# Compression blocks split straight from PSUM, and two element-wise steps moved to ScalarE

## Chip, cores, metric

One core of a Trainium2 chip. The metric is the device time of one execution in microseconds (us), the median over executions. TensorE (PE), VectorE (DVE), ScalarE (ACT), GpSimd (POOL) and SyncE (SP) each work through their own instruction list in order and wait for one another by semaphores; SP and ACT also start DMA transfers.

## What is computed

One layer of a hybrid transformer on 512 tokens of width 1024, all in float32. A mixer (sparse attention with compressed, selected and window branches, beside an mLSTM) is followed by cross-attention to 256 memory tokens and a SwiGLU network. The part around the change:

```python
def compress_blocks(kv, pos, w1, w2):               # blocks of 32 positions, stride 16
    c = kv.reshape(B, H, S // 16, 16, DH)           # 31 blocks come of 512 positions
    blocks = jnp.concatenate([c[:, :, :-1], c[:, :, 1:]], axis=3) + pos
    hid = jax.nn.silu(blocks.reshape(B, H, -1, 32 * DH) @ w1)
    return hid @ w2

def hybrid_mixer(h, ...):
    (nq, kc, vc, ksl, vsl, kwn, vwn, gt, mq, mk, mv, mi, mf, mo) = jnp.split(h @ w_in, IN_OFFSETS, axis=-1)
    k_cmp = compress_blocks(kv_heads(kc), cmp_pos_k, cmp_w1_k, cmp_w2_k)
    v_cmp = compress_blocks(kv_heads(vc), cmp_pos_v, cmp_w1_v, cmp_w2_v)
    o = native_sparse_attention(q, k_cmp, v_cmp, ...)
    qk = silu(causal_depthwise_conv([mq, mk], conv_w, conv_b))   # 4 taps
    hm = mlstm_chunkwise(mq, mk, mv, mi, log_sigmoid(mf))        # 4 heads
    hm = rms_norm_per_head(hm) * mlstm_norm
    y_ml = sigmoid(mo) * hm
    return jnp.concatenate([y_nsa, y_ml], axis=-1) @ w_out
```

## The kernel before

A float32 product is made of three matmuls of parts: each operand is split into a high part (a ScalarE copy, L166) and a low part (a subtraction, L167, on VectorE or GpSimd), and `mm3` (L292 to L295) multiplies low by high, high by low and high by high.

The in-projection h @ w_in is made in tiles of 128 output columns by 512 tokens. `dense_tiles` takes for each a PSUM bank of the tag "d" (`bk_dT`), of which there are **two**, runs 24 matmuls of 512 columns into it (8 slices of depth, three each), and hands the bank to an evacuation function. Its weights are split for two tiles at a time into `whi` and `wlo`. The order in which tiles and other work are written is a string of the table PLAN, and it begins

```python
"order": "c0 Lk c0 Lv kc m0 m0 Ck Ck Ck Ck c1 kc S0 O0 c1 S1 Cv Cv Cv Cv m2 S2 m2 O2 ks O1 ks q0 S3 q0 O3",
```

Here c0 and c1 are pairs of tiles for the convolution, kc is the pair of tiles of the compression's keys and values (the first kc is k, the second v), m0 and m2 are the output gate's tiles, Ck and Cv quarters of the compression's first product, S and O the scores and outputs of an mLSTM head. A scheduler of the framework then fixes the order of each engine's list and gives each tile its bank; a bank that is taken again waits until its last reader is done. What the engines carry out is that fixed order.

The functions that the change touches, by the line numbers of the profile:

- `ev_conv` (L654 to L667) evacuates a tile of the convolution: ScalarE copies the bank to `u` (L659), VectorE makes the first tap `zc = u*w3 + b` (L660) and adds three shifted taps (L663); ScalarE takes tanh (L665), VectorE finishes the silu (L666).
- `ev_mo` (L669 to L675) evacuates the output gate: ScalarE takes tanh from the bank (L673, `sg`), VectorE makes (sg + 1) * gain (L674).
- `ev_kcvc` (L751 to L770) builds the compression's blocks: two zeroed tiles `Xr`, eight additions of the positions from the bank (L761, 64 x 8 x 31 each), and four splits of `Xr` into `Xb` (L166, L167). The block dimension has 32 columns for 31 blocks, the last left zero.
- `comp` (L821 to L835) multiplies `Xb` by the split weights `w1s` (L830, 16 matmuls of 512 columns into `bk_hb`); `comp_out` (L837 on) adds two halves of the result through a matmul with the constant `fold`.

`mlstm_scores` (L687 to L718) stands beside them: it stacks q and k (`qm`, `kmA`, `kmB`), fetches a row broadcast over the partitions by a DMA that ScalarE starts (`rb`, L697), lets GpSimd add the causal mask (`dg`, L699), and ScalarE takes ten exponentials of pieces of `rb` and `dg` (L714, `sT`), which VectorE multiplies with the scores (L716). Later, `compressed` (L616 to L650) makes the softmax `pc` of the compressed branch on VectorE from PSUM and the bias tiles `nB`, which are fetched by DMA into tiles that the scores `sT` held before.

Of the kernel before, what the change touches and what calls it, by code (L numbers as in the profile page):

```python
# [8 lines left out]
F32 = mybir.dt.float32  # L9
F32R = mybir.dt.float32r  # L10
AF = mybir.ActivationFunctionType
OP = mybir.AluOpType
AX = mybir.AxisListType

P = 128
# [31 lines left out]
def hybrid_layer(ctx, tc, a, out):  # L47
# [39 lines left out]

# [34 lines left out]
    def engines(name):  # L122
        return [ENG[c] for c in PLAN[name]]
# [13 lines left out]
    def slot(shape, dt=F32, name="slot"):  # L137
        return sl.tile(shape, dt, tag="S", name=name)

    def gran(shape=(P, 512), dt=F32, name="gran"):  # L140
        return gp.tile(list(shape), dt, tag="G", name=name)
# [7 lines left out]
    def sgran(shape=(P, 512), dt=F32, name="s"):  # L149
        return gp.tile(list(shape), dt, tag="s", name=name, bufs=8)  # L150
# [10 lines left out]
    def small(shape, name, bufs=2):  # L161
        return sm.tile(shape, F32, tag=name, name=name, bufs=bufs)

    def split(hi, lo, src, eng=None, scale=None):
        if scale is None:
            first = nc.scalar.activation(hi, src, AF.Copy)  # L166
            second = (eng or nc.vector).tensor_tensor(lo, src, hi.bitcast(F32), op=OP.subtract)  # L167
        else:
            first = nc.scalar.activation(hi, src, AF.Copy, scale=scale)
            second = nc.vector.scalar_tensor_tensor(lo, src, scale, hi.bitcast(F32), op0=OP.mult, op1=OP.subtract)  # L170
        return first.ins, second.ins
# [277 lines left out]
    def cw(c, w):  # L449
        return chan[:, 4 * w + c:4 * w + c + 1]  # L450

    def cb(c):
        return chan[:, 16 + c:17 + c]

    def hn(c):
        return chan[:, 20 + c:21 + c]
# [197 lines left out]
    def ev_conv(base):  # L654
        def f(j, b):
            c = base + j
            u = gran(name="u")
            y = zc[c] = gran(name="zc")
            nc.scalar.activation(u, b, AF.Copy)  # L659
            nc.vector.tensor_scalar(y, u, cw(c, 3), cb(c), op0=OP.mult, op1=OP.add)  # L660
            for w in range(3):
                d = 3 - w
                nc.vector.scalar_tensor_tensor(y[:, d:512], u[:, 0:512 - d], cw(c, w), y[:, d:512],  # L663
                                               op0=OP.mult, op1=OP.add)
            nc.scalar.activation(u, y, AF.Tanh, scale=0.5)  # L665
            nc.vector.scalar_tensor_tensor(y, u, 1.0, y, op0=OP.add, op1=OP.mult)  # L666
        return f  # L667

    def ev_mo(base):  # L669
        def f(j, b):  # L670
            c = base + j
            sg[c] = gran(name="sg")
            nc.scalar.activation(sg[c], b, AF.Tanh, scale=0.5)  # L673
            nc.vector.tensor_scalar(sg[c], sg[c], 1.0, hn(c), op0=OP.add, op1=OP.mult)  # L674
        return f  # L675


# [71 lines left out]
    Xb = {}  # L749

    def ev_kcvc(j, b):  # L751
        n = "kv"[j]
        Xr = [sgran((P, 8, 64), name="Xr") for _ in range(2)]
        for X in Xr:
            nc.gpsimd.memset(X, 0.0)
        for kv in range(2):
            for r in range(2):
                full = b[64 * kv:64 * kv + 64, :].rearrange("p (b j r) -> p r j b", r=2, j=8)
                pt = posT[n][64 * r:64 * r + 64, :]
                for q in range(2):  # L760
                    nc.vector.tensor_tensor(Xr[q][64 * r:64 * r + 64, :, 32 * kv:32 * kv + 31],  # L761
                                            full[:, r, :, q:q + 31],
                                            pt[:, 8 * q:8 * q + 8].rearrange("p (j o) -> p j o", o=1).to_broadcast([64, 8, 31]),
                                            op=OP.add)
        Xb[n] = []
        for X in Xr:
            for g in range(2):
                B = gran((P, 4, 2, 64), F32R, name="Xb")
                split(B[:, :, 0, :], B[:, :, 1, :], X[:, 4 * g:4 * g + 4, :], engines("xb")[g])
                Xb[n].append(B)  # L770

    def dup(A, src, s=1.0):
        for r in (0, 64):
# [37 lines left out]
    hb, w1r = {}, {}  # L811
    fold = cst.tile([P, 64], F32, name="fold")
    nc.vector.tensor_tensor(fold, ident[:, 0:64], ident[:, 64:128], op=OP.add)

    def comp_load(n, g):
        w1r[n, g] = [ygran((P, 2, 256), name="w1") for _ in range(4)]
# [4 lines left out]
    def comp(n):  # L821

        hb[n] = bank("sc", "bk_hb")
        for s in range(8):
            take = x4 if PLAN["w1t" + n][s] == "T" else w4
            w = take([P, 2, 2, 256], F32R, name="w1s")
            split(w[:, :, 0, :], w[:, :, 1, :], w1r[n, s // 4][s % 4], engines("w1" + n)[s])
            for k in range(2):
                kk = 2 * s + k
                nc.tensor.matmul(hb[n], lhsT=Xb[n][kk // 4][:, kk % 4].rearrange("p q b -> p (q b)"),  # L830
                                 rhs=w[:, k].rearrange("p q c -> p (q c)"), start=kk == 0, stop=kk == 15)
            if s == 7:
                comp_out(n)
            if s % 2:
                yield  # L835
# [567 lines left out]
```

## Time and profile before

| | |
|---|---|
| median of 3 runs | 849.34 us (847.7, 849.34, 850.01) |
| the profiled execution's own time | 851.17 us |
| its span in the profile | 849.4 us |
| outside the span | 1.8 us |
| PE, DVE, ACT, POOL busy in the span | 819.2, 545.8, 422.3, 302.0 us |
| mean granted clock of TensorE | 0.992 of full speed |

The profiled execution is 1.8 us above the median of the runs. In the rows of the profile, a line number is that of the kernel before, `out<-in` are the program's names, and idle time is the engine's own, with what ended it. Matmuls overlap, so one that lasts 0.39 us may follow the one before by 0.23 us.

### The profile page before, as it was taken

The numbers are of one execution on the slowest core, as the hardware profiler recorded it, in microseconds if no ns is written. First come the engines' busy times: TensorE is split into PE (matmuls) and PEld (weight loads), VectorE is DVE, ScalarE is ACT, GpSimd is POOL, SyncE is SP. The second block draws the span as 40 slices with busy tenths as digits, with TensorE's granted clock in tenths as the row PEclk, the third lists the DMA queues.
The fourth block names the chain that finished last, engine by engine and source line by source line (L and its number), as shares of the span: only waits on it lengthen the run. The fifth ranks groups of instructions, "written<-read, shape, count | busy, mean of one in ns | idle before, by whom it ended". The sixth has DMA issues, their size and how long they took to land.

```text
span 849.4 us, 12651 instructions
## 1 busy us (share of the span) xinstructions
PE 819.2 (96%) x4841; PEld 703.4 (83%) x4841; DVE 545.8 (64%) x933; ACT 422.3 (50%) x837; POOL 302.0 (36%) x224
## 2 busy tenths in 40 slices
PE   8999989998999999999999999999999999999997
PEld 5776767885688978778888889999999999888885
DVE  6639596688879835743453769988877885224423
ACT  5513565757867743743452556444444444324311
POOL 3223342255437542411320111444444444323420
PEclk9999998999999999999999999999999999999999
DMA  8372222421202232251441033333333322223102
GB/s 260 109 226 73 62 66 70 136 69 51 66 11 88 91 137 84 60 189 50 141 155 51 1 124 103 118 113 110 114 113 112 110 104 100 100 100 99 50 25 75
DMA packets 67763, 83.18 MB, mean 98 GB/s; under 512 B 4368, under 2 KB 53873, under 8 KB 67702
## 3 DMA queue, kind: packets, MB, share of 16 engines
q1 hardware_dynamic: 64574, 77.97, 28.5%
q10 hardware_dynamic: 3128, 4.40, 1.6%
q8 instruction: 38, 0.62, 0.3%
q14 instruction: 23, 0.19, 0.1%
HBM read 80.24 MB, written 2.12 MB: 97 GB/s over the span
## 4 chain that ended last, share of the span: by engine, by line
PE 81%; DVE 10%; ACT 5%; issue 2%; POOL 1%; DMA 0%; DVEq 0%; ACTq 0%; POOLq 0%; SPq 0%
PE bk_X L1251 5%; PE bk_X L1252 5%; PE bk_X L1253 5%; PE bk_dT L293 5%; PE bk_ff L294 5%; PE bk_ff L295 5%; PE bk_ff L293 5%; PE bk_dT L294 5%; PE bk_dT L295 5%; PE bk_pv L977 3%; PE bk_dN L294 3%; PE bk_dN L293 3%; PE bk_dN L295 3%; PE bk_Z L1251 2%; PE bk_Z L1253 2%; PE bk_Z L1252 2%
## 5 line engine op out<-in xcount | busy, mean ns | idle before, releaser
L166 ACT ACTIVATE whi<-raw 128x1024 fp32r<-128x1024 f32 (+1 forms) x80 | 76.8, 967 | 66.6 <-PE bk_dT L293 28.4
L167 DVE TENSOR_TENSOR wlo<-raw,whi 128x1024 fp32r<-128x1024 f32 x41 | 55.9, 1367 | 78.4 <-PE bk_ff L294 43.0
L167 POOL TENSOR_TENSOR wlo<-raw,whi 128x1024 fp32r<-128x1024 f32 x23 | 55.9, 2429 | 102.2 <-ACT whi L166 100.3
L166 ACT ACTIVATE wh<-raw 128x1024 fp32r<-128x1024 f32 x64 | 67.2, 1056 | 49.5 <-PE bk_X L1251 17.8
L167 POOL TENSOR_TENSOR wl<-raw,wh 128x1024 fp32r<-128x1024 f32 x19 | 55.5, 2919 | 97.3 <-ACT wh L166 69.9
L293 PE MATMUL bk_dT<-hTh,wlo 128*128 128x512 f32 x192 | 77.5, 404 | 2.3 <-DVE Xr L761 1.1
L294 PE MATMUL bk_dT<-hTl,whi 128*128 128x512 f32 x192 | 76.7, 400 | 0.0
L295 PE MATMUL bk_dT<-hTh,whi 128*128 128x512 f32 x192 | 76.5, 398 | 0.0
L167 DVE TENSOR_TENSOR wl<-raw,wh 128x1024 fp32r<-128x1024 f32 x45 | 65.6, 1464 | 9.4 <-ACT wh L166 9.4
L167 POOL TENSOR_TENSOR gs<-gf,gs 128x512 fp32r<-128x512 f32 x22 | 33.6, 1536 | 64.7 <-ACT gs L166 64.7
L1252 PE MATMUL bk_X<-A,wh 128*128 128x256 f32 x192 | 54.6, 284 | 1.0 <-DVE A L167 1.0
L1251 PE MATMUL bk_X<-A,wl 128*128 128x256 f32 x192 | 54.4, 283 | 0.4 <-ACT A L166 0.4
L1253 PE MATMUL bk_X<-A,wh 128*128 128x256 f32 x192 | 54.3, 283 | 0.0
L294 PE MATMUL bk_ff<-wlo,gs 128*128 128x512 f32 x128 | 49.8, 389 | 0.0
L295 PE MATMUL bk_ff<-whi,gs 128*128 128x512 f32 x128 | 49.6, 389 | 0.0
L1251 PE MATMUL bk_X<-AS,wl 128*128 128x256 f32 x160 | 45.6, 285 | 2.7 <-ACT u L1306 2.6
L293 PE MATMUL bk_ff<-whi,gs 128*128 128x512 f32 x128 | 47.4, 389 | 0.0
L293 PEld LDWEIGHTS bk_dT<-hTh,wlo 128*128 128x128 f32 x192 | 36.5, 190 | 11.7 <-DVE wlo L167 2.1
L947 POOL TENSOR_SCALAR s<-s,acf 128x128 f32<-128x128 f32 (+3 forms) x32 | 36.3, 1146 | 25.6 <-PE bk_tr L962 15.9
L1252 PE MATMUL bk_X<-AS,wh 128*128 128x256 f32 x160 | 44.9, 281 | 0.0
L1253 PE MATMUL bk_X<-AS,wh 128*128 128x256 f32 x160 | 44.9, 281 | 0.0
L1251 PE MATMUL bk_Z<-AS,wl 128*128 128x256 f32 x160 | 44.9, 281 | 0.0
(374 smaller groups left out, 2533.3 us busy)
## 6 DMA issues: line engine op xcount, KB each, us to landing
raw<-in_w_gate_up_dram SPq DMA_DIRECT2D x22, 1024.0 KB, 5.7
raw<-in_w_down_dram SPq DMA_DIRECT2D x11, 1024.0 KB, 5.0
raw<-in_w_xkv_dram SPq DMA_DIRECT2D x8, 1024.0 KB, 5.1
raw<-in_w_in_dram SPq DMA_DIRECT2D x7, 1024.0 KB, 5.4
raw<-in_w_out_dram SPq DMA_DIRECT2D x4, 1024.0 KB, 5.1
raw<-in_w_xq_dram SPq DMA_DIRECT2D x4, 1024.0 KB, 5.2
raw<-in_w_xo_dram SPq DMA_DIRECT2D x4, 1024.0 KB, 5.1
raw<-in_w_in_dram SPq DMA_DIRECT2D x6, 512.0 KB, 4.0
```

Source lines behind the costliest of these rows:

```text
L166: first = nc.scalar.activation(hi, src, AF.Copy)
L167: second = (eng or nc.vector).tensor_tensor(lo, src, hi.bitcast(F32), op=OP.subtract)
L293: nc.tensor.matmul(o, lhsT=wl, rhs=xh, start=start, stop=False)
L294: nc.tensor.matmul(o, lhsT=wh, rhs=xl, start=False, stop=False)
L295: return nc.tensor.matmul(o, lhsT=wh, rhs=xh, start=False, stop=stop).ins
L947: ENG[on].tensor_scalar(s[:, 0:n], s[:, 0:n], c, None, op0=OP.mult)
L977: nc.tensor.matmul(o, lhsT=v, rhs=pTs[br][q][:, j], start=(br, j, q) == mms[0], stop=(br, j, q) == mms[-1])
L1251: nc.tensor.matmul(o, lhsT=wl[:, k, c], rhs=A.hi(n, k), start=st, stop=False, skip_group_check=True)
L1252: nc.tensor.matmul(o, lhsT=wh[:, k, c], rhs=A.lo(n, k), start=False, stop=False, skip_group_check=True)
L1253: nc.tensor.matmul(o, lhsT=wh[:, k, c], rhs=A.hi(n, k), start=False, stop=stop and k == 3, skip_group_check=True)
```

## The change

In the compression, `Xr` and its additions go. The bank itself is split: a view of it with overlapping blocks (31 columns at a stride of 16) is copied by ScalarE and subtracted by VectorE, 64 x 16 x 31 at a time, four of each for k and four for v, into one tile `Xb` from the pool `slot`. The positions are split into column 31, that of the missing block, and `fold` gets its row of that column added to all its columns, so that the positions' product reaches every block in the matmul that was there already. The first tap of the convolution and the scale of the output gate become activations on ScalarE. TensorE's matmuls are the same in number and shape. Line numbers behind the table are lower by 1, those behind `ev_kcvc` by 5.

```diff
--- before.py
+++ after.py
@@ -85,7 +85,6 @@
         "w1tk": "WTWTWTWW",
         "w1tv": "WWWWWWWW",
 
-        "xb": "vv",
         "c0": "pp",
         "c1": "vp",
         "m0": "pp",
@@ -657,7 +656,7 @@
             u = gran(name="u")
             y = zc[c] = gran(name="zc")
             nc.scalar.activation(u, b, AF.Copy)
-            nc.vector.tensor_scalar(y, u, cw(c, 3), cb(c), op0=OP.mult, op1=OP.add)
+            nc.scalar.activation(y, b, AF.Identity, scale=cw(c, 3), bias=cb(c))
             for w in range(3):
                 d = 3 - w
                 nc.vector.scalar_tensor_tensor(y[:, d:512], u[:, 0:512 - d], cw(c, w), y[:, d:512],
@@ -671,7 +670,7 @@
             c = base + j
             sg[c] = gran(name="sg")
             nc.scalar.activation(sg[c], b, AF.Tanh, scale=0.5)
-            nc.vector.tensor_scalar(sg[c], sg[c], 1.0, hn(c), op0=OP.add, op1=OP.mult)
+            nc.scalar.activation(sg[c], sg[c], AF.Identity, scale=hn(c), bias=hn(c))
         return f
 
 
@@ -749,25 +748,18 @@
     Xb = {}
 
     def ev_kcvc(j, b):
+
         n = "kv"[j]
-        Xr = [sgran((P, 8, 64), name="Xr") for _ in range(2)]
-        for X in Xr:
-            nc.gpsimd.memset(X, 0.0)
+        X = Xb[n] = slot([P, 2, 8, 2, 64], F32R, name="Xb")
+        nc.gpsimd.memset(X[:, :, :, :, 63:64].bitcast(F32), 0.0)
+        pos = posT[n].rearrange("p (q j o) -> p q j o", q=2, o=1)
+        split(X[:, :, :, 0, 31:32], X[:, :, :, 1, 31:32], pos)
         for kv in range(2):
             for r in range(2):
-                full = b[64 * kv:64 * kv + 64, :].rearrange("p (b j r) -> p r j b", r=2, j=8)
-                pt = posT[n][64 * r:64 * r + 64, :]
-                for q in range(2):
-                    nc.vector.tensor_tensor(Xr[q][64 * r:64 * r + 64, :, 32 * kv:32 * kv + 31],
-                                            full[:, r, :, q:q + 31],
-                                            pt[:, 8 * q:8 * q + 8].rearrange("p (j o) -> p j o", o=1).to_broadcast([64, 8, 31]),
-                                            op=OP.add)
-        Xb[n] = []
-        for X in Xr:
-            for g in range(2):
-                B = gran((P, 4, 2, 64), F32R, name="Xb")
-                split(B[:, :, 0, :], B[:, :, 1, :], X[:, 4 * g:4 * g + 4, :], engines("xb")[g])
-                Xb[n].append(B)
+                one = b[64 * kv:64 * kv + 64, r:r + 1]
+                full = bass.AP(tensor=one.tensor, offset=one.offset, ap=[one.ap[0], [16, 2], [2, 8], [16, 31]])
+                to = X[64 * r:64 * r + 64, :, :, :, 32 * kv:32 * kv + 31]
+                split(to[:, :, :, 0], to[:, :, :, 1], full)
 
     def dup(A, src, s=1.0):
         for r in (0, 64):
@@ -811,6 +803,9 @@
     hb, w1r = {}, {}
     fold = cst.tile([P, 64], F32, name="fold")
     nc.vector.tensor_tensor(fold, ident[:, 0:64], ident[:, 64:128], op=OP.add)
+    every = small([P, 1], "every", 1)
+    nc.vector.tensor_copy(every, fold[:, 31:32])
+    nc.vector.tensor_scalar(fold, fold, every, None, op0=OP.add)
 
     def comp_load(n, g):
         w1r[n, g] = [ygran((P, 2, 256), name="w1") for _ in range(4)]
@@ -827,7 +822,7 @@
             split(w[:, :, 0, :], w[:, :, 1, :], w1r[n, s // 4][s % 4], engines("w1" + n)[s])
             for k in range(2):
                 kk = 2 * s + k
-                nc.tensor.matmul(hb[n], lhsT=Xb[n][kk // 4][:, kk % 4].rearrange("p q b -> p (q b)"),
+                nc.tensor.matmul(hb[n], lhsT=Xb[n][:, kk // 8, kk % 8].rearrange("p q b -> p (q b)"),
                                  rhs=w[:, k].rearrange("p q c -> p (q c)"), start=kk == 0, stop=kk == 15)
             if s == 7:
                 comp_out(n)
```

The scheduler orders the lists anew. Three places differ where the text below speaks of them.

**ScalarE, around the evacuation of the first tile of m0** (`sg<-bk_dT`). Before:

```order
L665 ACTIVATE u<-zc 128x512
L166 ACTIVATE Xb<-Xr 128x4x64 x4
L774 ACTIVATE kmA<-zc 64x512 x2
L697 DMA rb<-rd 128x512
L166 ACTIVATE w1s<-w_689 128x2x256
L673 ACTIVATE sg<-bk_dT 128x512
L166 ACTIVATE w1s<-w_691 128x2x256
L714 ACTIVATE sT<-rb,ub 128x128 x3
```

Now:

```order
L664 ACTIVATE u<-zc 128x512
L165 ACTIVATE Xb<-bk_dT 64x16x31
L766 ACTIVATE kmA<-zc 64x512 x2
L696 DMA rb<-rd 128x512
L165 ACTIVATE Xb<-bk_dT 64x16x31
L713 ACTIVATE sT<-rb,ub 128x128 x3
L165 ACTIVATE Xb<-bk_dT 64x16x31
L165 ACTIVATE w1s<-w_692 128x2x256
L713 ACTIVATE sT<-dg,ub 128x128 x2
L713 ACTIVATE sT<-rb,ub 128x128 x2
L713 ACTIVATE sT<-dg,ub 128x128
L672 ACTIVATE sg<-bk_dT 128x512
```

The evacuation of m0's first tile, which stood ahead of the first exponentials `sT`, now stands behind eight of them, and two of the four splits of the bank stand between the rest.

**TensorE, the step from the first to the second tile of m0** (numbers tell tiles of one name apart; `bk_dT_820` and `bk_dT_811` are the first tile's bank, `bk_dT_852` and `bk_dT_843` the second's). Before:

```order
L293 MATMUL bk_dT_820<-hTh_93,wlo_817 128x512
L294 MATMUL bk_dT_820<-hTl_95,whi_816 128x512
L295 MATMUL bk_dT_820<-hTh_93,whi_816 128x512
L293 MATMUL bk_dT_852<-hTh_92,wlo_849 128x512 [waits DVE_49,Pool_49]
L294 MATMUL bk_dT_852<-hTl_94,whi_848 128x512 [waits Activation_49]
```

Now:

```order
L292 MATMUL bk_dT_811<-hTh_93,wlo_808 128x512
L293 MATMUL bk_dT_811<-hTl_95,whi_807 128x512
L294 MATMUL bk_dT_811<-hTh_93,whi_807 128x512
L292 MATMUL bk_dT_843<-hTh_92,wlo_840 128x512 [waits Activation_49,Pool_49]
L293 MATMUL bk_dT_843<-hTl_94,whi_839 128x512
```

The second tile waited for VectorE, namely the last `Xr` that reads kc's bank; now it waits for ScalarE, at the count that the evacuation `sg<-bk_dT` of m0's first tile reaches: the framework has given it the bank of the tile just ahead of it.

**VectorE, the softmax of the compressed branch** (`pc`, its row maxima `mn`, and `nB`, the last head's bias tile that the copy hands on). Before:

```order
L733 TENSOR_SCALAR hnat<-bk_mn,dn 128x128 [waits DVE_49]
L471 COPY nB<-nB 128x256 [waits DMAHW3_49]
L632 TENSOR_TENSOR pc<-bk_pc,nB 128x7 [waits PE_49,Pool_49]
L632 TENSOR_TENSOR pc<-bk_pc,nB 128x7
L632 TENSOR_TENSOR pc<-bk_pc,nB 128x7 [waits DMAHW6_49]
L632 TENSOR_TENSOR pc<-bk_pc,nB 128x7 [waits DMAHW7_49]
L632 TENSOR_TENSOR pc<-bk_pc,nB 128x15 x4
```

Now, behind the same additions:

```order
L636 TENSOR_REDUCE mn<-pc 128x16 [waits DVE_49]
L729 TENSOR_TENSOR dn<-bk_mn,dn 128x1 [waits DVE_49]
L730 RECIPROCAL dn<-dn 128x1 [waits DVE_49]
L470 COPY nB<-nB 128x256 [waits DMAHW3_49]
L637 TENSOR_TENSOR pc<-pc,mn 128x512 [waits DVE_49]
```

The copy, which waits for a DMA, stood ahead of all of the softmax and now stands between its maxima and its subtraction.

## Rows read from the trace of the kernel before

**Rows 1.** The page, part 1: busy us (share of the span) and instructions of each engine.

```profile
PE 819.2 (96%) x4841; PEld 703.4 (83%) x4841; DVE 545.8 (64%) x933; ACT 422.3 (50%) x837; POOL 302.0 (36%) x224
```

**Rows 2.** Windows: start:end, length, busy us of PE, PEld, DVE, ACT, POOL, clock, DMA share, GB/s.

```profile
80.00:90.00 10.00, 8.87 (x42) 7.06 (x43) 8.25 (x20) 6.21 (x15) 1.58 (x1) 1.00 0.47 131
90.00:100.00 10.00, 8.53 (x36) 6.09 (x35) 6.34 (x9) 6.14 (x13) 2.54 (x2) 1.00 0.05 5
...
110.00:120.00 10.00, 8.65 (x40) 6.43 (x39) 9.35 (x27) 7.77 (x24) 2.61 (x2) 1.00 0.22 59
120.00:130.00 10.00, 6.91 (x25) 3.83 (x24) 9.61 (x17) 7.12 (x15) 4.85 (x4) 0.81 0.00 1
130.00:140.00 10.00, 10.00 (x44) 8.26 (x45) 4.46 (x11) 5.96 (x17) 4.84 (x6) 0.85 0.40 131
...
190.00:200.00 10.00, 7.75 (x33) 5.29 (x31) 9.03 (x25) 6.35 (x16) 6.20 (x3) 0.83 0.01 2
...
250.00:849.40 599.40, 585.53 (x3683) 524.59 (x3681) 367.12 (x474) 277.73 (x472) 211.10 (x136) 1.00 0.29 96
```

**Rows 3.** Waits of PE from 70 to 210 us: total us, times, longest.

```profile
PE bk_hb L830 <- DVE w1s L167: 2.5, 3, 1.6
PE bk_sc L927 <- DVE mx L931: 1.4, 2, 1.1
PE bk_dT L293 <- DVE Xr L761: 1.1, 1, 1.1
...
PE bk_hb L830 <- DVE Xb L167: 1.0, 1, 1.0
```

**Rows 4.** Timeline of PE, 75 to 134 us: start, length, and in brackets idle time before.

```profile
83.90 0.47 PE L293 MATMUL bk_dT<-hTh,wlo 128*128 128x512 f32 x1 [1.09 <-DVE Xr L761]
...
89.54 1.10 PE L830 MATMUL bk_hb<-w1s,Xb 128*128 128x512 f32 x4
...
96.97 0.50 PE L293 MATMUL bk_dT<-hTh,wlo 128*128 128x512 f32 x1 [0.35 <-DVE wlo L167]
```

**Rows 5.** Timeline of ACT and its DMA queue, 79 to 98 us.

```profile
80.93 0.63 ACT L665 ACTIVATE u<-zc 128x512 f32<-128x512 f32 x1 [4.29 <-DVE zc L663]
...
84.58 0.37 ACTq L697 DMA_DIRECT2D rb<-rd  x1
...
86.53 0.58 ACT L673 ACTIVATE sg<-bk_dT 128x512 f32<-128x512 f32 x1
...
87.87 0.99 ACT L714 ACTIVATE sT<-rb,ub 128x128 f32<-128x128 f32 x3 [0.24 <-DMA rb<-rd]
```

**Rows 6.** DMA issues from 56 to 140 us: count, KB each, median us to landing.

```profile
rb<-rd ACTq DMA_DIRECT2D x3, 256.0 KB, 3.7
```

**Rows 7.** Timeline of POOL, 66 to 130 us.

```profile
87.92 1.58 POOL L699 TENSOR_TENSOR dg<-rb,cc 128x512 f32<-128x512 f32 x1 [8.10 <-DMA rb<-rd]
...
103.51 2.39 POOL L167 TENSOR_TENSOR wlo<-raw,whi 128x1024 fp32r<-128x1024 f32 x1 [7.67 <-ACT whi L166]
```

**Rows 8.** Timeline of DVE: around the first kc, and around the first tile of c1.

```profile
80.76 2.99 DVE L761 TENSOR_TENSOR Xr<-bk_dT,chan 64x248 f32<-64x248 f32 x8
...
104.05 3.52 DVE L660 TENSOR_SCALAR zc<-u,chan 128x512 f32<-128x512 f32 x1
```

**Rows 9.** Groups by shape, 56 to 130 us: count, busy us, mean ns, idle before.

```profile
L660 DVE TENSOR_SCALAR zc<-u,chan 128x512 f32<-128x512 f32 x4 | 7.5, 1864 | 1.7 <-ACT u L659 1.7
...
L716 DVE TENSOR_TENSOR sT<-sT,bk_ms 128x512 f32<-128x512 f32 x2 | 1.4, 683 | 0.0
L674 DVE TENSOR_SCALAR sg<-sg,chan 128x512 f32<-128x512 f32 x2 | 1.0, 482 | 0.0
```

**Rows 10.** Groups of ACT by shape, 56 to 130 us.

```profile
L714 ACT ACTIVATE sT<-rb,ub 128x128 f32<-128x128 f32 x12 | 4.1, 390 | 0.8 <-DMA rb<-rd 0.8
...
L659 ACT ACTIVATE u<-bk_dT 128x512 f32<-128x512 f32 x4 | 2.3, 578 | 0.0
```

**Rows 11.** DMA issues from 150 to 215 us.

```profile
nB<-fd SPq DMA_DIRECT2D x8, 128.0 KB, 4.7
```

## The prediction, made before the changed kernel ran

> **What bounds the kernel now.** I read the busy times first, then the span in windows, then the waits of TensorE, then the timelines around them. TensorE is busy for 819.2 of 849.4 us and VectorE, from which the change takes work, for 545.8 [rows 1]. So a faster VectorE is worth nothing by itself; it is worth the TensorE idle time that it ends. From 250 us on, where the change touches nothing, TensorE is busy 585.5 of 599.4 us. Ahead of that, the idle time of the five windows from 80 to 130 and 190 to 200 us that are not full is 1.13 + 1.47 + 1.35 + 3.09 + 2.25 = 9.3 us [rows 2]. Besides this, the granted clock is 0.81 and 0.85 of full in 120 to 140 us and 0.83 in 190 to 200 us: counted at the half level of 1.2 GHz that is 3.8 + 3.0 + 3.4 us of time on the low level, in which TensorE does half its work, so some 4 to 5 us are lost to it. These 13 to 14 us are all that there is to win here. The waits say for what: most of it for the split compression weights `w1s`, 2.5 us from VectorE alone; 1.1 us for the last `Xr`, 1.0 us for `Xb`, 1.4 us for the score maxima late in the stage [rows 3].
>
> **The operations themselves.** Off VectorE go four first taps of 1.86 us (7.5 us in all), four scales of 0.48 us (1.9 us) and sixteen additions, eight of which took 2.99 us; its eight low parts grow from about 0.37 us, the pace of those additions, which are of like size, to that of a 512-column read of PSUM, 0.68 us [rows 8, 9]. That is 7.5 + 1.9 + 6.0 - 2.5 = 13 us less. ScalarE gains eight activations and its eight high parts grow from 256 to 496 columns; by the 512-column copy from PSUM of 0.58 us, and at most half of it for the growth [rows 10], that is 8 x 0.58 + 8 x 0.29 = 7 us more. Both engines have room in the mean [rows 1], and the two added copies for `fold` at the start are under 0.3 us of VectorE behind other work. So these prices enter the sum only where an instruction stands ahead of something for which TensorE waits. ScalarE's price is the less certain. The row of the exponential with a per-partition operand gives 0.39 us for 128 columns where the copy of 512 without one takes 0.58 [rows 10], so an operand costs something; bounds for the new activations are 0.58 and, adding the shorter instruction's whole time, 0.97 us.
>
> The Trainium skill speaks against this part: "ScalarE: Activation LUTs", "Rules for kernel authors", sends multiplications and additions to VectorE, and "What ACT_TABLE_LOAD costs" on the same page charges some 93 ns for each per-partition operand, an estimate of 0.80 us for an activation of 512 columns with two of them. Eight at that price instead of 0.58 us would be 1.8 us more of ScalarE, none of it in the sum below, since none of the eight stands ahead of a wait of TensorE in the steps that follow.
>
> **The step that decides: the second tile of m0.** Before, this tile started at 83.90 us, after 1.09 us of waiting for the last `Xr` [rows 4]. Its end is at 89.54 us, 5.64 us later. By the new order it takes the bank of m0's first tile and waits for that bank's evacuation `sg`, and on ScalarE that evacuation stands behind eight exponentials; all need the DMA `rb`, and the last five stand at or behind the first that needs `dg`, which GpSimd makes of `rb`. The replay: the tanh of the second convolution tile ran at 80.93 to 81.56 us [rows 5]. I take it as unmoved. VectorE then was in the additions until 83.75 us [rows 8]; with these gone it finishes the silu at once, 0.7 us, and ScalarE's `kmA` and the DMA can go at about 82.2 us (82.6 if a first subtraction of `Xb` comes between, 81.7 at the earliest) instead of 84.58 us. From issue to the first exponential it took 87.87 - 84.58 = 3.29 us [rows 5], and the median of three such transfers is 3.7 us [rows 6]: landed at 85.5 to 85.9 us. `dg` takes GpSimd 1.58 us [rows 7]; ScalarE meanwhile makes three exponentials (0.99 us), a split of `Xb` and one of `w1s` (0.58 us each), 2.15 us, which ends later. So the first exponential of `dg` is at 87.6 to 88.0 us. Five exponentials at a pace of 0.3 us (three in 0.99 us) and `sg` of 0.58 us follow [rows 5]: 1.5 + 0.6 us. The bank is free at 89.7 to 90.1 us; with the bounds, and with `dg` as what counts, at 88.7 to 90.5. I take 89.7 us, **+5.8 us** (4.8 to 6.6). TensorE has nothing else in its list: it is idle for 6.9 us instead of 1.09 us.
>
> Two smaller terms follow. The clock: at 118 to 130 us TensorE was broken up, and the clock was at 0.81 of full in 120 to 130 and at 0.85 in 130 to 140 us, although TensorE was busy throughout the second [rows 2]: by that window, some 3.0 us of dense work passed at 1.2 GHz and cost 1.5 us. An idle time of 6.9 us in one piece is more broken than that stretch was, so I put **+1.5 us** on the start of the second tile (0 to 3).
>
> Given back: the quarters of Ck ran from 89.54 to the start of c1 at 96.97 us, 7.43 us [rows 4]. Their matmuls alone are sixteen of 512 columns at 0.23 us and 1.3 us of interleaved scores, 5.0 us. With TensorE 5 us late, the weights are ready, and nearly all of 7.43 - 5.0 = **-2.4 us** comes back (-1 to -2.4: two of the eight splits still stand behind the evacuation of m0's second tile).
>
> **Cv.** Before, its first matmul waited 1.0 us for `Xb` [rows 3]. Now the four high and four low parts write one tile and so follow one another: 4 x (0.58 + 0.68) = 5.0 us [rows 9, 10]. Before, 3.0 us of additions and a last low part of 0.4 us made that way [rows 8]. Counted from the start of c1, the first matmul is then some 1.6 us later than before. Against that, the first tap that held VectorE for 3.52 us at 104.05 us [rows 8] is gone, what stands behind it on VectorE comes up to 3.52 - 0.48 = 3 us earlier, and the waits for `w1s` shrink, of which 2.5 + 1.0 us is all that can vanish. I take **+0.5 us** at the start of m2 (-2 to +2.5).
>
> **The compressed softmax, 184 to 200 us.** TensorE idles 2.25 us here before, at a clock of 0.83 [rows 2]. Now the copy of `nB` stands ahead of the softmax's subtraction. The DMA it waits for takes 4.7 us [rows 11] and can start only when the last head's outputs have released their tile, which TensorE now does later. The wait is moved, not clearly lengthened: between 24 matmuls that can cover it (24 x 0.23 = 5.6 us) and 4.7 us of DMA with some 3.5 us of softmax behind it, the gap is 2.6 us, near the 2.25 us of before. I take **0** (-2 to +4, the upper end a DMA laid bare).
>
> **The sum**, against the profiled execution's own 851.17 us: 5.8 + 1.5 - 2.4 + 0.5 + 0 = +5.4, so 856.6 us. That execution lies 1.8 us above the median of the runs; from the median it is 849.3 + 5.4 = **854.7 us**, slower by 0.6%. A measurement of this kernel can tell about 0.3%, 2.5 us, from no change.
>
> **The rivals.**
>
> *The relief arrives (faster).* If `sg` is not held back, because the exponentials find `rb` landed when ScalarE reaches them, m0's second tile starts at about 83.9 us as before. Then Ck gains what `w1s` waits allow, Cv loses its 1.0 us, and with fewer breaks the clock's fall at 126 us is mostly saved: -1 - 1 - 2.5 = -4.5 us, 844.9 us. It turns on one point: the DMA would have to land by about 83 us, within 1 us of its issue, against 3.3 and 3.7 us in the rows; or, failing that, Ck and Cv must give back everything. What speaks for it: VectorE was held for 3.52 us on a first tap that began at 104.05 us while GpSimd's subtraction ran from 103.51 us [rows 7, 8], and four such taps took 1.86 us in the mean where the scale of the same width takes 0.48 us [rows 9]. The change takes these away, so VectorE's later work comes 1 to 3 us sooner. The Trainium skill, "SBUF — State Buffer", "SBUF: two separate sides", calls this an exclusive lock of a port that VectorE and GpSimd share; the rows of the first tap agree (3.52 us against 0.48). Chance 0.17.
>
> *It is absorbed (no change).* The stall at m0 is there, but the clock stays up, Ck gives back 2.4 us and the Cv stage the rest of it, because its `w1s` waits and its low clock (some 3 us together) go when all its inputs are early: 5.8 - 2.4 - 3 = +0.4, 849.7 us, and anything within 2.5 us. For it speaks that these waits stand behind exactly the work that VectorE loses; against it, the serial `Xb`. Chance 0.21.
>
> *Both stalls (slower still).* The low clock lasts through Ck, and the copy of `nB` lays its DMA bare: 5.4 + 1.5 + 4 = +10.9 us, 860.2 us. It is the upper part of the forecast's side. Chance 0.14, and 0.48 for the forecast itself.
>
> *The change doesn't do what it says.* ScalarE could be slower on the strided view of the bank than on a plain one: at 0.97 instead of 0.58 us, four serial parts would put 1.6 us more on Cv, 856.3 us, inside the forecast.
>
> **The numbers.** Slower by over 0.3%: 0.48 + 0.14 = 0.62. Within 0.3%: 0.21. Faster: 0.17. The range from 846 to 861 us holds the forecast's bounds, the absorbed case whole, the case of both stalls up to 1 us beyond its price, and of the faster case only its weaker part; about 0.18 is left out. The forecast's own range is 851.8 to 859.5 us.
>
> **What would show it.** Right: TensorE idle for 5 to 8 us before the second tile of m0, ended by ScalarE's `sg`, with the exponentials just ahead of it; a granted clock below 0.9 in the 10 us behind; hardly a wait inside Ck; the first Cv matmul waiting for `Xb`; busy times of VectorE near 533 us and of ScalarE near 429 us. Wrong: `sg` ahead of the exponentials in time, that is a transfer `rb` of under 1 us; or TensorE with no wait over 2 us before 100 us. In the first case the faster rival holds. If the stall is there and the total is still at 849 us, Cv has paid for it, and its `w1s` waits will be gone.

## The result, and the profile after

The changed kernel took **857.52 us** in the median of four runs (856.22 to 858.86), the kernel before 849.67 us beside it: slower by a factor of 1.0086, 95% interval 1.0067 to 1.0105. The prediction was 854.7 us, slower, with a range of 846 to 861 us. The profiled execution has a span of 856.7 us against 849.4 us, so the two profiles differ by 7.3 us, and where these lie can be read from TensorE's timeline. The table gives the start of the first matmul of each step.

| step | before, us | after, us | later by | that step adds |
|---|---|---|---|---|
| second tile of m0 | 83.90 | 89.89 | 5.99 | 5.99 |
| Ck (ends the tile above) | 89.54 | 97.86 | 8.32 | 2.33 |
| c1 (ends Ck) | 96.97 | 103.12 | 6.15 | -2.17 |
| Cv | 119.57 | 125.54 | 5.97 | -0.18 |
| m2 (ends Cv) | 129.76 | 135.70 | 5.94 | -0.03 |
| first transposes of `pc` | 196.37 | 202.40 | 6.03 | 0.1 |
| last transposes of `pc` | 250.0 | 259.0 | 9.0 | 3.0 |
| end of the span | 849.4 | 856.7 | 7.3 | -1.7 |

The page of the changed kernel, part 1, in the columns of [rows 1]:

```profile
PE 815.8 (95%) x4841; PEld 701.8 (82%) x4841; DVE 537.4 (63%) x913; ACT 431.9 (50%) x847; POOL 302.9 (35%) x222
```

VectorE lost 8.4 us of work and ScalarE gained 9.6 us; TensorE's matmuls are as many as before. The windows of the changed kernel, to be read against [rows 2]:

```profile
80.00:90.00 10.00, 3.36 (x19) 2.58 (x19) 4.85 (x9) 7.24 (x17) 1.26 (x1) 0.91 0.49 131
90.00:100.00 10.00, 10.00 (x34) 7.97 (x35) 2.06 (x3) 4.64 (x10) 0.56 (x1) 0.75 0.00 0
...
120.00:130.00 10.00, 7.05 (x36) 5.07 (x34) 8.28 (x20) 7.33 (x19) 3.92 (x4) 1.00 0.00 1
130.00:140.00 10.00, 7.58 (x22) 4.80 (x23) 8.37 (x10) 5.47 (x9) 3.81 (x3) 0.83 0.22 57
...
200.00:210.00 10.00, 8.21 (x33) 6.26 (x34) 8.44 (x32) 8.04 (x21) 5.09 (x4) 0.66 0.33 104
```

In 80 to 90 us TensorE works for 3.36 us where it worked for 8.87, and the 10 us behind that run at 0.75 of the clock, all of them busy. The second loss is in 200 to 210 us, at a clock of 0.66, where the kernel before had 0.83 in 190 to 200 us [rows 2]. The waits of TensorE from 70 to 220 us, in the columns of [rows 3]:

```profile
PE bk_dT L292 <- ACT sg L672: 6.6, 1, 6.6
PE bk_sc L922 <- DVE mx L926: 4.9, 3, 1.9
PE bk_mt L741 <- DVE hnat L740: 1.5, 1, 1.5
PE bk_hb L825 <- POOL w1s L166: 1.4, 2, 0.9
PE bk_dT L292 <- DVE wlo L166: 1.1, 1, 1.1
PE bk_hb L825 <- DVE Xb L166: 1.0, 1, 1.0
...
PE bk_hb L825 <- DVE w1s L166: 0.5, 1, 0.5
```

The wait for `Xr` of 1.1 us has become one of 6.6 us for ScalarE's evacuation `sg`; the waits for VectorE's `w1s` fell from 2.5 to 0.5 us, which is the relief that was meant; a wait of 1.5 us for `hnat` stands in Cv, where there was none; the scores near 200 us wait 4.9 instead of 1.4 us. How the first came about stands in ScalarE's timeline, against [rows 5]:

```profile
80.93 0.63 ACT L664 ACTIVATE u<-zc 128x512 f32<-128x512 f32 x1 [4.49 <-DVE zc L662]
...
82.38 0.37 ACTq L696 DMA_DIRECT2D rb<-rd  x1
...
85.55 0.98 ACT L713 ACTIVATE sT<-rb,ub 128x128 f32<-128x128 f32 x3 [1.47 <-DMA rb<-rd]
86.56 0.58 ACT L165 ACTIVATE Xb<-bk_dT 64x496 fp32r<-64x496 f32 x1
...
88.73 0.39 ACT L713 ACTIVATE sT<-dg,ub 128x128 f32<-128x128 f32 x1
89.14 0.60 ACT L672 ACTIVATE sg<-bk_dT 128x512 f32<-128x512 f32 x1
```

ScalarE waits for the DMA, makes eight exponentials and two splits, and only then empties the bank for which TensorE has waited since 83 us. TensorE's timeline, against [rows 4]:

```profile
89.89 0.77 PE L292 MATMUL bk_dT<-hTh,wlo 128*128 128x512 f32 x1 [6.61 <-ACT sg L672]
...
97.86 2.02 PE L825 MATMUL bk_hb<-w1s,Xb 128*128 128x512 f32 x8
...
103.12 0.50 PE L292 MATMUL bk_dT<-hTh,wlo 128*128 128x512 f32 x1
```

Ck, which took 7.43 us, now runs in 5.26 us without a wait. In the softmax near 195 us, VectorE and then GpSimd show:

```profile
193.61 1.09 DVE L470 COPY nB<-nB 128x256 f32<-128x256 f32 x1 [0.97 <-DMA nB<-fd]
194.62 2.89 DVE L637 TENSOR_TENSOR pc<-pc,mn 128x512 f32<-128x512 f32 x1
```

```profile
194.50 2.47 POOL L166 TENSOR_TENSOR wlo<-raw,whi 128x1024 fp32r<-128x1024 f32 x1
```

The copy waits for its DMA and takes 1.09 us, and the subtraction behind it then falls into a long subtraction on GpSimd and lasts 2.89 us, to 0.5 us after GpSimd's end, where the same line took 0.69 us before. The two met in the kernel before as well, but there VectorE began first, by 0.01 us, and GpSimd's subtraction lasted 2.92 us:

```profile
189.72 0.69 DVE L638 TENSOR_TENSOR pc<-pc,mn 128x512 f32<-128x512 f32 x1
189.73 2.92 POOL L167 TENSOR_TENSOR wlo<-raw,whi 128x1024 fp32r<-128x1024 f32 x1
```

### The profile page after: what moved, and what is told of

Same layout as the page of the kernel before. It is cut to its first block, busy times and chain, and to the rows that moved or that the text cites. A ratio compares the mean times of both kernels' runs of the same rounds, so it can differ in the third digit from the quotient of the medians.

```text
span 856.7 us, 12631 instructions
## 1 busy us (share of the span) xinstructions
PE 815.8 (95%) x4841; PEld 701.8 (82%) x4841; DVE 537.4 (63%) x913; ACT 431.9 (50%) x847; POOL 302.9 (35%) x222
## 4 chain that ended last, share of the span: by engine, by line
PE 78%; DVE 11%; ACT 5%; issue 2%; POOL 1%; DMA 1%; ACTq 0%; DVEq 0%; POOLq 0%
PE bk_X L1246 5%; PE bk_ff L292 5%; PE bk_ff L294 5%; PE bk_ff L293 5%; PE bk_X L1247 5%; PE bk_dT L292 5%; PE bk_X L1248 5%; PE bk_dT L293 4%; PE bk_dT L294 4%; PE bk_pv L972 3%; PE bk_dN L293 3%; PE bk_dN L292 3%; PE bk_dN L294 3%; PE bk_Z L1246 2%; PE bk_Z L1248 2%
## 5 line engine op out<-in xcount | busy, mean ns | idle before, releaser
L928 ACT ACTIVATE s<-s,mx 128x128 f32<-128x128 f32 (+3 forms) x64 | 35.6, 558 | 18.4 <-DVE mx L926 17.9
L1247 PE MATMUL bk_Z<-AS,wh 128*128 128x256 f32 x160 | 44.3, 277 | 0.0
```

The costliest lines, as they stand in the source:

```text
L928: nc.scalar.activation(s[:, 0:n], s[:, 0:n], AF.Exp, bias=mx, scale=-1.0, accum_out=sums[:, br, hh:hh + 1])
L1247: nc.tensor.matmul(o, lhsT=wh[:, k, c], rhs=A.lo(n, k), start=False, stop=False, skip_group_check=True)
```

## The experiments

Ratios are to the kernel before, run beside each, with 95% intervals.

**1. The blocks alone.** The first tap and the gate's scale go back to VectorE:

```diff
-            nc.scalar.activation(y, b, AF.Identity, scale=cw(c, 3), bias=cb(c))
+            nc.vector.tensor_scalar(y, u, cw(c, 3), cb(c), op0=OP.mult, op1=OP.add)
...
-            nc.scalar.activation(sg[c], sg[c], AF.Identity, scale=hn(c), bias=hn(c))
+            nc.vector.tensor_scalar(sg[c], sg[c], 1.0, hn(c), op0=OP.add, op1=OP.mult)
```

> The blocks are split straight from the bank as in the change; the first tap and the scale of the output gate stay on VectorE. ScalarE's order around the first tile of m0 is that of the change, with the evacuation behind eight exponentials. Theory (place in the order): the whole loss comes with this half; idle time of TensorE before the second tile of m0 of 6 to 7 us, ended by ScalarE's sg, and a total of 855 to 858.5 us, +6 to +9 over the kernel before. Rival (load of ScalarE): the eight activations that ScalarE took over are what costs; without them the total falls back to 852 us or less.

Measured: 861.59 us, 1.0141 (1.0126 to 1.0156), slower than the whole change. The stall at m0 is there as expected, and the rival, by which ScalarE's eight activations cost the time, is refuted: without them it is worse. But the total is above the range. TensorE's waits show a part of why:

```profile
PE bk_dT L292 <- ACT sg L672: 6.6, 1, 6.6
PE bk_sc L922 <- DVE mx L926: 5.0, 3, 1.9
PE bk_hb L825 <- DVE Xb L166: 3.5, 1, 3.5
```

Cv waits 3.5 us for `Xb` instead of 1.0 us. With the first taps on VectorE (1.90 us each in this run) the serial parts of `Xb` for v are late; the taps' move hid that. Of these 2.5 us, 1.4 are left at the start of m2 (137.10 against 135.70 us); the rest of the 4.1 us by which this run is slower than the change is not accounted for.

**2. ScalarE's part alone**, the opposite half, on the kernel before.

> The first tap and the scale of the output gate go to ScalarE as in the change; the blocks are built on VectorE as before. In the order the evacuation of m0's first tile stays ahead of the exponentials, and m0's second tile waits for VectorE's last Xr as before. Theory: wait before the second tile of m0 at 1 to 1.5 us, total within 847 to 851 us, near the kernel before; it may be up to 2 us faster, since a first tap of 3.5 us on VectorE is gone. Rival (load of ScalarE): 852 us or more.

Measured: 851.79 us, 1.0031 (1.0017 to 1.0044): between the two theories, just slower than before. The stall at m0 is absent (its second tile starts without a wait) and the order keeps the evacuation early. The first taps' relief is real: c1 starts at 94.85 us, 2.1 us sooner than before. It is then lost in two places, of which the first is this:

```profile
118.02 1.53 PE L830 MATMUL bk_hb<-w1s,Xb 128*128 128x512 f32 x4 [2.70 <-DVE Xb L167]
```

Ahead of the low parts VectorE has the same large steps as before, but three of them now begin just behind an operation of GpSimd:

```profile
106.70 1.66 DVE L695 SCALAR_TENSOR_TENSOR kmB<-zc,kmA 64x512 fp32r<-64x512 f32 x1
108.39 1.81 DVE L666 SCALAR_TENSOR_TENSOR zc<-u,zc 128x512 f32<-128x512 f32 x1
...
115.78 1.50 DVE L779 SCALAR_TENSOR_TENSOR qm<-zc,qm 64x512 fp32r<-64x512 f32 x1
```

```profile
106.31 1.50 POOL L699 TENSOR_TENSOR dg<-rb,cc 128x512 f32<-128x512 f32 x1 [1.15 <-DMA rb<-rd]
108.36 1.29 POOL L167 TENSOR_TENSOR w1s<-w,w1s 128x512 fp32r<-128x512 f32 x1 [0.55 <-ACT w1s L166]
115.42 1.32 POOL L167 TENSOR_TENSOR w1s<-w,w1s 128x512 fp32r<-128x512 f32 x1 [5.76 <-issue]
```

Each ends 0.5 to 0.6 us after GpSimd's; before, they took 0.69, 0.69 and 0.68 us. So of 2.1 us only 0.4 us are left at m2 (129.33 us), and 2.3 us more are lost between the first and last transposes of `pc` (196.54 and 252.47 us, against 196.37 and 250.00); there the granted clock is 0.86 and 0.80 in 190 to 210 us, against 0.83 and 1.00 before. Work taken off VectorE ahead of a stage did not stay won here. The halves don't add up: 1.4% and 0.3% make 0.9% together.

**3. The evacuation first.** The changed kernel, with the first head's exponentials queued behind the tanh of m0's first tile:

```diff
+                if h == 0:
+                    with tc.issue_after(mo_tanh[0]):
+                        nc.scalar.activation(W[:, c:c + 128], src, AF.Exp, bias=ub[:, idx[i, j], h:h + 1])
...
```

> The changed kernel with one edit: the exponentials of the first mLSTM head are queued behind the tanh of m0's first tile on ScalarE. Nothing is computed differently. Theory: TensorE's wait before the second tile of m0 falls from 6.6 to under 1.5 us and the low clock behind it goes; Ck then waits again for the weights (its 2.4 us are lost), so the total falls by 5 to 7 us to 850.5 to 852.5 us; the wait near 200 us stays. Rival (the wait only changes its name): with sg early the next thing that is late, the serial Xb or kc's bank, holds TensorE for as long; total 855 us or more.

Measured: 854.94 us, 1.0058 (1.0037 to 1.0078): a gain of 2.6 us, half of what was expected, and a total at the rival's bound of 855 us. But the wait did not change its name, as the rival had it: it fell from 6.6 to 3.4 us, not under 1.5, and it is still one for `sg`:

```profile
84.48 0.58 ACT L165 ACTIVATE Xb<-bk_dT 64x496 fp32r<-64x496 f32 x1 [0.73 <-DVE Xb L166]
84.96 0.62 ACT L165 ACTIVATE w1s<-w 128x512 fp32r<-128x512 f32 x1
85.61 0.60 ACT L672 ACTIVATE sg<-bk_dT 128x512 f32<-128x512 f32 x1
```

So the exponentials were one half of what stood ahead of `sg`; the other half are `kmA`, a part of `w1s` and the splits of kc's bank, of which the third waits 0.73 us for VectorE's low part. The theory had to be widened: not only the place of one instruction, but the turns between the two engines.

**4. The copy of the bias tile.** The changed kernel with `"bias": "vaappaap"` for `"vaappavp"`: ScalarE copies the seventh head's tile.

> The changed kernel with one letter of a table altered: the copy of the bias tile of the seventh head is made by ScalarE instead of VectorE, so it no longer stands ahead of the softmax's subtraction. Theory (the copy's wait for its DMA holds the softmax): TensorE's idle time between 190 and 220 us falls from 5.5 to 2 to 3 us, and the total by 2 to 3.5 us, to 854 to 855.5 us; the stall at m0 stays at 6 to 7 us. Rival (the softmax is late because the outputs of the last head are late): total within 1 us of the change, 856.5 to 858.5 us.

Measured: 855.63 us, 1.0072 (1.0057 to 1.0087), 1.9 us below the change, just outside the expected range; the stall at m0 stays (7.0 us). TensorE's idle time from 190 to 220 us fell from 5.5 to 4.2 us, not to the 2 to 3 us expected. The last transposes of `pc` start at 256.4 instead of 259.0 us, while m0 is as late as in the change. The subtraction is now

```profile
194.22 1.66 DVE L637 TENSOR_TENSOR pc<-pc,mn 128x512 f32<-128x512 f32 x1
```

so it is over 1.6 us sooner: it starts 0.4 us sooner, and GpSimd holds it for 1.0 instead of 2.2 us. The granted clock did not fall here either:

```profile
200.00:210.00 10.00, 7.43 (x41) 5.05 (x42) 8.25 (x32) 8.52 (x26) 6.00 (x5) 1.00 0.32 106
```

That the copy stood in the way is shown by its removal; how much of the 2.6 us is the copy's wait, its falling in with GpSimd, and the clock (1.00 for 0.66), is not separated. Nor does this run alone show that the copy's new place is to blame: run 8 moves it in the kernel before.

**5. High parts first.** The changed kernel, with the four splits written as four high and then four low parts:

```diff
+        lows = []
...
-                split(to[:, :, :, 0], to[:, :, :, 1], full)
+                nc.scalar.activation(to[:, :, :, 0], full, AF.Copy)
+                lows.append((to, full))
+        for to, full in lows:
+            nc.vector.tensor_tensor(to[:, :, :, 1], full, to[:, :, :, 0].bitcast(F32), op=OP.subtract)
```

> The changed kernel with its four splits of the bank written in another order: four high parts on ScalarE, then four low parts on VectorE, instead of high and low in turn. In the order the evacuation of m0's first tile is ahead of the exponentials again, m0's second tile waits for VectorE's last low part (kc's bank), and the copy of the seventh head's bias tile is ahead of the softmax as before the change. Theory (the turns between the engines made the order bad): TensorE's wait before the second tile of m0 is 3 to 4 us (high parts end at 83.7, low parts 2.5 us later), the wait near 200 us falls back to 2 to 3 us, and the total is 850.5 to 853.5 us. Rival (the price of reading the bank on both engines): 855 us or more, near the change.

Measured: 853.69 us, 1.0037 (1.0021 to 1.0054), 0.2 us above the expected range, and below the rival's 855 us. TensorE's idle time from 190 to 220 us is 3.9 us, not the 2 to 3 us expected (2.7 before, 5.5 in the change). The same work on the same engines; only the turns are gone, and with them the order with `sg` behind the exponentials and the copy amid the softmax. TensorE's wait before m0's second tile is now for the low parts:

```profile
86.40 0.77 PE L292 MATMUL bk_dT<-hTh,wlo 128*128 128x512 f32 x1 [3.44 <-DVE Xb L766]
```

**6. The splits early.** Besides, the tanh of the second convolution tile (and the step behind it) is written after the high parts and queued behind them:

```diff
+            def rest():
+                nc.scalar.activation(u, y, AF.Tanh, scale=0.5)
+                nc.vector.scalar_tensor_tensor(y, u, 1.0, y, op0=OP.add, op1=OP.mult)
+            if c == 2:
+                owed.append(rest)
...
+        if owed:
+            with tc.issue_after(hi):
+                owed.pop()()
```

> As the run with the high parts first, and the tanh of the second convolution tile is written behind them, so that ScalarE splits kc's bank in the 4.5 us in which it waited for VectorE before that tanh. Theory (ScalarE's order, not its load): high parts end at about 79 us, low parts run on VectorE from 80.8 to 83.3 us, TensorE waits 0 to 1 us before the second tile of m0, the clock stays up there, and the total is 847 to 851 us. Rival (the later work pays it back: the tanh, rb and the scores of the first head are 2 to 3 us later and hold Ck or c1): 852 us or more.

Measured: 849.5 us, 0.9995 (0.9982 to 1.0008), as the theory had it. ScalarE, and TensorE:

```profile
76.35 2.35 ACT L769 ACTIVATE Xb<-bk_dT 64x496 fp32r<-64x496 f32 x4
80.64 0.63 ACT L666 ACTIVATE u<-zc 128x512 f32<-128x512 f32 x1 [1.94 <-DVE zc L663]
```

```profile
83.34 0.47 PE L292 MATMUL bk_dT<-hTh,wlo 128*128 128x512 f32 x1 [0.36 <-DVE Xb L775]
```

kc's last matmul ended near 75.8 us, and in the change ScalarE stood in front of it for 4.49 us, waiting for VectorE's third tap, with the splits queued behind. Used for the splits, that idle time takes the stall away but for 0.36 us, and the total can't be told from the kernel before.

**7 and 8. The copy moved there, and in the kernel before**, by the letter of run 4.

> As the run before it, with the copy of the seventh head's bias tile on ScalarE. Theory: VectorE loses a wait and a copy ahead of the softmax; 0 to 2 us faster than without, 846 to 850 us. Rival: the copy was hidden in this order; within 0.5 us of the run without.

> The kernel before with only the copy of the seventh head's bias tile on ScalarE, as a control for that edit. Theory: as the copy took 1.44 us of VectorE ahead of the softmax, 0 to 1.5 us faster, 848.3 to 849.8 us. Rival: the order of the whole list changes with it and decides more than the copy; a total off by over 2 us either way.

Measured: 848.89 us, 0.9983 (0.9974 to 0.9993), and 849.22 us, 0.9984 (0.9971 to 0.9996). These two are the only versions below the kernel before, both by less than 0.2%. Run 7 is 0.6 us below run 6, between the theory and the rival, and its profile speaks for the rival: up to the last transposes of `pc` the two are alike (250.1 and 250.3 us). In the kernel before, the letter brings the first transposes from 196.4 to 194.3 us, and run 8's total is as its theory had it. So the letter is worth about as much there (0.16%) as on the change (0.14%, from 1.0086 to 1.0072), and run 7's lead of 0.17% over the kernel before can be the letter's alone.

**9 and 10. The mLSTM's outputs moved back**, on run 7:

```diff
-        "order": "... c1 kc S0 O0 c1 S1 Cv Cv Cv Cv m2 ...",
+        "order": "... c1 kc S0 c1 Cv S1 Cv O0 Cv Cv m2 ...",   (9)
+        "order": "... c1 kc S0 c1 S1 Cv Cv Cv Cv O0 m2 ...",   (10)
```

> As the run with Xb early and the copy on ScalarE, and the table's order is altered: the second mLSTM head's scores stand behind the first quarter of Cv and the first head's outputs behind the second, so their small steps no longer stand ahead of the split weights of Cv on ScalarE. Theory (the rest of the idle time in Cv, 2.2 us for VectorE's w1s and 1.1 us for hnat, comes from those steps standing in the way): the w1s wait falls under 1 us, total 845 to 848 us. Rival: the outputs are only late elsewhere, at m2 or at the scores near 200 us; 848.5 us or more.

> As the run with Xb early and the copy on ScalarE, and the first mLSTM head's outputs stand behind all of Cv in the table's order. Theory: Cv runs without a wait for w1s over 1 us, total 845 to 848 us. Rival: the outputs come in m2's time and the tiles of their scores come free later, so the bias tiles near 200 us are late; 849 us or more.

Measured: 850.77 us, 1.0017 (1.0002 to 1.0032), and 851.49 us, 1.0031 (1.0015 to 1.0047). Both rivals hold; within Cv, too, waits for `w1s` of 2.6 us (run 9) and 1.6 us (run 10) stay, where under 1 us was expected. In run 10 the last Cv matmul starts at 124.8 instead of run 7's 129.2 us, and the time is spent again where the softmax is awaited. That wait is nearly the same in both (4.6 and 4.4 us); run 9's:

```profile
PE bk_pcT L646 <- DVE pc L643: 4.6, 1, 4.6
```

## Why the prediction was right, and where it was off

**The step that decides** was right in mechanism and size: m0's second tile waits for `sg` behind the exponentials, +5.99 us where +5.8 was forecast. `rb` was issued at 82.38 us (forecast 82.2) and could be used after 3.2 us; the first exponential of `dg` was at 87.56 us (87.6). The relief of VectorE did not reach it, as its list still waited at the same place. Runs 3, 5 and 6 show the cause, and show it to be wider than the prediction had it. The bank's evacuation was late through the order of ScalarE's list, and that order came from writing high and low parts in turn into one tile: run 5 alters nothing else. Runs 5 and 6 remove the stall in two halves (6.61, 3.44, 0.36 us) without moving any work off ScalarE.

**The clock** was under-sized: +2.33 us for +1.5. The second tile of m0 took 7.97 us where it took 5.64 before. At half pace, as the prediction counts, the 2.33 us are 4.7 us at the low level instead of the 3.0 us taken from the window behind the earlier fall; that fall had 3.8 us more in the window ahead, which were left out.

**Given back in Ck**: -2.17 for -2.4 us, right; Ck ran without a visible wait.

**Cv**: -0.2 for +0.5 us, within its bounds, but not for the reasons given. The first matmul was to come 1.6 us later, counted from the start of c1; it came 0.2 us sooner, and its wait for `Xb` is 1.0 us as before. Run 1 shows that the taps' move paid for the serial parts: without it the wait is 3.5 us. Behind that matmul the waits did not shrink: those for `w1s` from both engines fell from 2.5 to 1.8 us, those for `hnat` and `wlo` grew from 0.6 to 2.5 us. What made up for it is, as far as the windows show, the clock: 1.00 over Cv instead of 0.83 (119.57 to 129.76 us before, 125.54 to 135.70 us now), up to 1.8 us at half pace, of which the term had nothing. That the sum came out near zero is luck. Nor were the waits before mostly for `w1s`: they were 3.6 of the 9.3 us, GpSimd's share of 1.1 us included.

**The compressed softmax** is the term that was mis-sized: forecast 0 (-2 to +4), measured +3.1 (+0.1 up to the first transposes, +3.0 behind them). The prediction said that the wait was moved, not clearly lengthened, and counted the DMA and the softmax's usual 3.5 us. What it left out is that a subtraction moved by 5 us can begin behind a long one on GpSimd: 2.89 for 0.69 us. The rows had shown that for a first tap [rows 7, 8]. The Trainium skill, "SBUF — State Buffer", "SBUF: two separate sides", cited for the faster rival, says that a VectorE operation with two inputs in that memory contends with a GpSimd operation that reads it. The trace agrees (2.89 us, and 0.69 us where VectorE began first). It was weighed for the work that the change takes away and not for the work that it moves. The term left out the clock too: by the windows' 0.66 and 0.83, some 6.8 us at the low level instead of 3.4.

The runs show the cause of the +3.1 us only in part. From m2 to the last transposes the kernel before takes 120.2 us, run 8 118.8, the change 123.3 and run 4 120.4. So with the copy on ScalarE in both, 1.6 us of the 3.1 are still there, and at most 1.5 come of the copy's new place and of what it brings about; what the 1.6 us are stays open. In runs 1 and 3 the subtraction took 2.90 us again, and the stretch 123.4 us; but run 2 needs 123.1 us with a subtraction of 0.69.

**What no term covered**: from the last transposes to the end, the changed kernel gains 1.7 us, spread over 600 us in which the same instructions run. In the profiles of all runs this stretch takes 596.5 to 599.4 us, and runs 6 and 7, which differ by the one letter, are 2.2 us apart in it; its cause stays open. With the terms as measured, 5.99 + 2.33 - 2.17 - 0.2 + 3.1 - 1.7 = 7.3 us, for +5.4 forecast. That the total is this near is in part luck, as the gain without a term stands against the loss in the softmax.

**The prices**: an activation with a per-partition scale and bias takes 0.77 us from PSUM and 0.81 us from SBUF (means of four and two), between the bounds of 0.58 and 0.97. The estimate of 0.80 us from the Trainium skill, "ScalarE: Activation LUTs", "What ACT_TABLE_LOAD costs", was the better value, and no step of the sum depended on it. VectorE's saving was 8.4 us for 13 forecast: the operations counted did fall by 12.6 us, but the softmax's subtraction took 2.2 us more; the rest is spread over many groups. The shifted taps changed little in sum (14.5 for 14.0 us): the one that now comes first took 6.2 us in four instead of 3.0, the others less.

**The rivals.** The faster one needed `rb` within 1 us of its issue; it took 3.2 us. The absorbed one failed with Ck alone giving back. "Both stalls", 860.2 us, held in part: the second stall was there, at three quarters of its price, but the low clock did not last through Ck, whose sixteen matmuls and scores took 5.26 us, near the 5.0 us of the dense pace. The forecast's own range, 851.8 to 859.5 us, holds the measured time; its upper end follows from no term of the sum.

## What to carry to other kernels

When a scheduler writes the lists, price the new order and not only the operations: find each instruction that frees a PSUM bank, and look for what in front of it waits for a DMA or for another engine's turn. Two engines that fill one tile in turn make a chain that pulls other work in between; all of one engine's parts first, then all of the other's, kept the list in its old order (3.8 us here, run 5). Taking work off an engine that isn't the bound gave nothing by itself: with the stall removed, the change measured 0.9995 of the time before. And a list that moves by a few us meets other work on the engines beside it: a VectorE step that began 0.1 us behind GpSimd's took 2.89 us, and 0.69 us where it began 0.01 us ahead.

## What the runs showed of the hardware

A DMA was issued ahead of activations that stand before it in ScalarE's list. In the kernel before, `rb` stands behind both `kmA` and was issued at 84.58 us [rows 5], while they ran from 84.70 us:

```profile
84.70 1.27 ACT L774 ACTIVATE kmA<-zc 64x512 fp32r<-64x512 f32 x2
```

In the changed kernel it was issued at 82.38 us, 0.06 us after the first `kmA` began, which had waited 0.29 us for VectorE; the second ran from 82.98 us. So in these two lists `rb` was not held by the time that the activations ahead of it take; in the changed one it went as soon as their wait was over.

A VectorE operation that began within 0.5 us behind one on GpSimd ended 0.5 to 0.6 us after it, in five cases: the softmax's subtraction (2.89 us; 1.66 us in run 4) and run 2's three steps (1.66, 1.81 and 1.50 us), each of which takes 0.68 or 0.69 us alone.
